# Values of three slots and one gate's columns in Strassen pairs, and the last attention beside the second gate

## The chip, the cores and the metric

The kernel runs on one core of a Trainium2 chip. Its engines work side by side, each through its own list of instructions in order: TensorE (PE in the profile; its weight loads are PEld) multiplies matrices, VectorE (DVE) and ScalarE (ACT) work on elements, GpSimd (POOL) and SyncE (SP) here only issue DMA transfers. An engine waits for another through semaphores. Matmuls write to PSUM, which has eight banks of 128 x 512 float32 values; everything else lies in SBUF. The metric is the device time of one execution in microseconds (us); the time before is 1420.82 us, the median of three runs from 1420.28 to 1421.73.

## The reference

One layer of a decoder on 256 tokens of width 2048, in float32:

```python
u = rmsnorm(h, g_mix_pre)
proj = u @ w_in        # q, k, v of 12 + 4 heads of 128, and two gates of 2048 columns
ya = dilated_mixture_attention(q_a, k_a, v_a) @ w_branch_a   # 3 groups of 4 heads, softmax
yb = stick_breaking_attention(q_b, k_b, v_b) @ w_branch_b    # 4 heads
mix = (sigmoid(gate_a) * ya + sigmoid(gate_b) * yb) @ w_out
h = h + rmsnorm(mix, g_mix_post)
f = (gelu(conv(u2 @ w_up)[:5632]) * conv(u2 @ w_up)[5632:]) @ w_down   # u2 = rmsnorm(h)
h = h + rmsnorm(f, g_ffn_post)
h = h + sigmoid(h @ w_ple_gate) * (p @ w_ple_in)
```

The heads are taken in four slots: slot s has head s of each of the three dilated groups and head s of the stick-breaking branch, so that each slot has four q columns, four k columns and four v columns, each 128 wide.

## The kernel before

**Products in three parts.** Every float32 factor is split into a high part that TensorE takes at full rate and a low remainder; a product is high x high + high x low + low x high. The weights come from HBM as one stream of items, each 128 x 1024 (eight blocks of 128 x 128) in the order in which TensorE uses them. For an item SP loads `raw` (five buffers), ScalarE makes the high part (`high`, line 246) and VectorE the low part (`low`, line 312), into a ring of seven buffers.

**Order.** The order of the work is written out by hand. TensorE asks for the next item, which calls `tick(i)`; there the work that was put off with `defer` is issued, one stage of each waiting job per tick, then the high part of item i + 6, then the low parts up to item i + 5, and then the deferred work of VectorE (it goes ahead of the low parts only when more than two jobs still wait in the list). `lows` also issues the loads, up to five raw buffers ahead of what has been split.

**Strassen pairs.** Where a group has eight columns of 128, two tiles of the inner dimension (k1, k2), two halves of the tokens and two halves of the columns make a 2 x 2 by 2 x 2 product. `gate_groups` (Winograd's form of Strassen) does it in 7 instead of 8 products of 128 x 128 x 512. It needs four combinations of token tiles, made once by `combine(p)` and used by every gate group, and two sums of weights per pair: an item of the first sum, which comes by DMA (SP loads one summand, POOL adds the other; `add_ahead`, `sum_to`, lines 279 and 285), and an item of the second sum, which VectorE makes of it (lines 265 and 266, `weight_sums`). Their lows are line 306. The sums by DMA are put into free quarters of `gh`, the room of the transposed input x. At the end joins (line 995) put the seven products together.

**The stages around the change.** For each slot: eight columns of q and k (`mm`, lines 393 and 395; a column takes one of four PSUM banks in turn, and its evacuation `qk_evac` is deferred), then the four columns of v (`v_units`, lines 725 to 727, with tokens as the stationary side), which are evicted at once by ScalarE and VectorE. The attention of a slot is a generator of eight steps. Six are called between the k-tiles of the slot's v (`STEPS`), two in the next slot's columns (`PACE`); for slot 0 it is two and six. After slot 3 come the first four columns of gate a, beside which the last attention ends, and of gate b (`by_token`), the combinations, the branches' projections, and then three gate groups of eight columns, each with four pairs and eight plain k-tiles. The output projection has a group of its own with six pairs; the token sums of its pairs are made by `gathered(p)`, and the weight sums by `sum_early`.

**Banks.** While attention runs, four banks (`pm1`) serve the columns in turn, and four (`pat`: `S` of two banks, `po`, `z`) serve attention.

Of the kernel before, what the change touches and what calls it, by code (L numbers as in the profile page):

```python
# [14 lines left out]
T = 256  # L15
# [3 lines left out]
NS = 4  # L19
# [15 lines left out]
PAIRS = 4  # L35
OUT = 6
# [4 lines left out]
TURNED = {("qk", s, 1): 3 for s in (2, 3)}  # L41
# [3 lines left out]
STEPS = [(11, 15)] + [(1, 3, 3, 11, 11, 15)] * 3  # L45
PACE = {1: (1, 1, 2, 2), 2: (2,), 3: (2,)}


def _plan():
# [19 lines left out]

    for s in range(NS):  # L70
# [6 lines left out]
    o = 3 * (WA + WB)  # L77

    for j in range(0, KT, 4):
        gates = [[("w_in", o + kind * KT + n) for n in range(j, j + 4)] for kind in range(2)]  # L80
        if j == 0:
            add(("ga", j), gates[0], KT, single)
# [44 lines left out]
def _pairs(group):  # L127

    key = group[0]
    if key[:2] == ("pairs", "out"):  # L130
        return OUT
    if key[0] == "gates" or key[:2] == ("pairs", "pg"):
        return PAIRS
# [3 lines left out]
def _plain():  # L137
    return [k for k in range(KT) if k % 8 >= PAIRS]
# [10 lines left out]
def hybrid_block_kernel(ctx: ExitStack, tc: tile.TileContext, head, gx, xt, pT, convp, bias, masks, gains, w, out):  # L149
# [21 lines left out]
    for g in _plan():  # L171
        if g[0] == "pad":
            short.append(used // 8)
        if _pairs(g):
            assert used % 8 == 0
            before = 14 - 2 * _pairs(g) if g[0][:2] in (("pairs", "pg"), ("pairs", "out")) else 0
            while len(stream) < used // 8 + before + 2 * len(sums_of):
                stream.append(len(stream) - 2 * len(sums_of))
            for p in range(_pairs(g)):
# [3 lines left out]
                if g[0][0] == "pairs" and p < DSUM[g[0][1]]:  # L183
                    early_sums.append(i)
# [6 lines left out]
    gate_sums = sorted(sums_of)[:3 * PAIRS]  # L191
# [56 lines left out]
    def weight_sums(i):  # L248
# [4 lines left out]
        if i not in raw:  # L253
            if n == 0 or a in by_dma:
                x = mps["mp"].tile([128, 1024], F32, name="wsum", tag="wsum")
# [13 lines left out]
    def add_ahead(*ms):  # L269


        for m in ms:
            if m < len(gate_sums):
                k = (4, 12, 0, 8)[m % PAIRS]
                sum_to(gate_sums[m], gh[:, G + k * T:G + (k + 4) * T])
# [26 lines left out]
    def low(i, a=0, b=1024, src=None):  # L302
        if i in sums:
# [3 lines left out]
            if sums[i][1] and sums[i][0] in gate_sums:  # L307
                add_ahead(gate_sums.index(sums[i][0]) + PAIRS)
# [181 lines left out]
    pTs = keep.tile([128, 2, 2 * T], F32R, name="pTs")  # L490
# [224 lines left out]
    def v_units(s):  # L715
        biases[s] = ab.tile([128, 1152], F32, name="bi")
        nc.sync.dma_start(biases[s], bias[s])
        pv = [bank() for _ in range(2)]
# [21 lines left out]
    def attention(s):  # L740
# [10 lines left out]
        P = []  # L751
        for t in range(2):
# [8 lines left out]
            e = ab.tile([128, 3 * n], F32, name=f"e{t}")  # L761
# [78 lines left out]

    def att_step():
# [24 lines left out]
    gates = {}  # L866
    pt = [temp("t", 2) for _ in range(2)]
    for k in range(2):
        nc.sync.dma_start(pt[k], pT[:, k])
        defer((None, None), (None, None), (lambda k=k: usplit(pTs, k, pt[k], low=False), lambda k=k: ulow(pTs, k, pt[k])))  # L870
# [29 lines left out]
    def turn_merged(j, o):  # L900
# [7 lines left out]
        def part(low):  # L908
            for n in range(2):
# [7 lines left out]
    idt = tmp.tile([128, 128], F32, name="idt", tag="ga", bufs=3)  # L917
# [3 lines left out]

    spare = [("s", 2), ("s", 2), ("gb", LATE + 1), ("gb", LATE + 1), ("gb", LATE + 1),
             ("ga", LATE + 1), ("ga", LATE + 1), ("t1", 2), ("t1", 2),
             ("ln", 1), ("ms", 1), ("t", 2), ("t", 2),
             ("s2", 2), ("s2", 2), ("y", 1)]
    S1, S2, S3, S4, A22 = range(5)
    comb, halves_of = [], []

    def combine(p):
        ks, y = (p, p + 8), []  # L930

        def act():
            y.append(mp.tile([128, 6, 128], F32, name="comb"))
            for n, k in enumerate(ks):
                ACT.activation(y[0][:, (5, S4)[n]], h[:, k, :H], AF.Copy, scale=gain(0, k))

        def dve():
            x = y[0]
            DVE.scalar_tensor_tensor(x[:, S3], h[:, ks[0], H:], gain(0, ks[0]), rho, op0=OP.mult, op1=OP.mult)
            DVE.scalar_tensor_tensor(x[:, A22], h[:, ks[1], H:], gain(0, ks[1]), rho, op0=OP.mult, op1=OP.mult)  # L940
            DVE.tensor_tensor(x[:, S1], x[:, S3], x[:, A22], OP.subtract)
            DVE.tensor_tensor(x[:, S2], x[:, S1], x[:, 5], OP.subtract)
            DVE.tensor_tensor(x[:, S3], x[:, 5], x[:, S3], OP.subtract)
            DVE.tensor_tensor(x[:, S4], x[:, S2], x[:, S4], OP.add)
            p == PAIRS - 1 and add_ahead(*range(2, PAIRS))

        def split(low):
            for n in range(4):
                if not low:
                    if not halves_of:  # L950
                        tag, bufs = spare.pop(0)
                        x = tmp.tile([128, 2, 1 + (tag in ("s2", "t")), 128], F32R, name="sp", tag=tag, bufs=bufs)
                        halves_of.extend(x[:, :, i] for i in range(x.shape[2]))
                    comb[p].append(halves_of.pop(0))
                    ACT.activation(comb[p][n][:, 0], y[0][:, n], AF.Copy)
                else:
                    DVE.tensor_tensor(comb[p][n][:, 1], y[0][:, n], f(comb[p][n][:, 0]), OP.subtract)
        comb.append([])
        defer((act, dve), (lambda: split(False), lambda: split(True)))

    def three_wide(ps, x, w, first=False, last=False):
        for n, (i, j) in enumerate(((0, 0), (0, 1), (1, 0))):
            PE.matmul(ps, x[i], w[j], start=first and n == 0, stop=last and n == 2, skip_group_check=True)  # L963

    def gate_groups(j, merged):
# [4 lines left out]

        def tokens(k, t):
            return [u[:, k, i * T + t * H:i * T + (t + 1) * H] for i in range(2)]
# [88 lines left out]
    for j in range(0, KT, 4):  # L1061
        if j:
            ga, gb = gate_groups(j, merged)
        else:
            for kind in ("ga", "gb"):
                ps = [bank() for _ in range(2)]
                for _ in by_token((kind, j), ps, u, (2, 2) if kind == "ga" else ()):
                    att_step()
                if kind == "ga":
                    while stages:  # L1070
                        att_step()
                    at_sc.close()
                    pat_sc.close()
                    pm_sc, pm = scope("pm", space=PSUM)
                    banks["of"] = [(pm1, 4), (pm, 4)]
                    banks["n"] = 0
                    mg_sc, mp = scope("mp")
                    mps["mp"] = mp
                    mg = mp.tile([128, KT, 2 * T], F32R, name="mg")
                    ga = gate("ga", ps)  # L1080
                    rho = tmp.tile([128, H], F32, name="rho", tag="y")
                    DVE.reciprocal(rho, R[:, :H])
# [636 lines left out]
```

## Time and profile before

| | |
|---|---|
| median of three runs | 1420.82 us (1420.28 to 1421.73) |
| profiled execution, its time | 1420.48 us |
| its span | 1418.7 us |
| PE, DVE, ACT, POOL busy | 1412.8, 1188.6, 867.7, 74.7 us |
| slot 1: columns, values | 73.9 to 122.8 us, 122.8 to 148.7 us |
| slots 2 and 3, values | 195.5 to 221.3 us, 268.1 to 294.0 us |
| first columns of the gates | 294.0 to about 338 us |
| three gate groups (with the branches between them) | 350.9 to 497.8 us |
| output projection | from 508.7 us |

A row of the timeline reads: start in us, length in us, engine, line, operation, what is written <- what is read, shape, count; in brackets the idle time of the engine ahead of it and what ended that. A row of a table by stage has the stage's bounds and length, and each engine's busy time with its number of instructions, TensorE's clock, the share of time in which the DMA engines were busy, and what they moved. A row of the view of waits gives who waited for whom, in total, how often, and the longest. A wait is put down to what came last by the profile.

### The profile page before, as it was taken

The page shows a single profiled execution, that of the slowest core. Times are in us where ns is not written, and L with a number is a line of the kernel's source. Part 1 is how long each engine was busy: PE and PEld are TensorE (multiplying, and loading weights), DVE is VectorE, ACT ScalarE, POOL GpSimd, SP SyncE. Part 2 cuts the span into 40 slices and gives each one's busy share as a digit, 9 for nine tenths or more (in the row PEclk, how much of TensorE's full clock was granted, in tenths as well). Part 3 has the DMA queues.
Part 4 walks back from the last instruction along what each step waited for, and adds up shares of the span by engine and source line. Part 5 has one row for each costly group of instructions (what it writes and reads, how often), then busy time and mean ns, then how long its engine had stood idle before and what let it go on. Part 6 is the DMA issues. An engine that isn't in the chain of part 4 may idle for free.

```text
span 1418.7 us, 20516 instructions
## 1 busy us (share of the span) xinstructions
PE 1412.8 (100%) x7343; PEld 1209.5 (85%) x7343; DVE 1188.6 (84%) x1865; ACT 867.7 (61%) x1319; POOL 74.7 (5%) x89
## 2 busy tenths in 40 slices
PE   9999999999999999999999999999999999999998
PEld 8888888888888887898888888888888888888887
DVE  7876666568898899879999788997889978899798
ACT  7665555466656657666666566655566556566564
POOL 0000000002110020000000010000000001000000
PEclk9999999999999999999999999999999999999999
DMA  7754746469976796877876886377863778728775
GB/s 290 268 172 153 250 150 222 152 218 268 298 222 218 254 289 163 299 265 232 254 210 214 266 263 214 102 259 239 260 221 101 248 251 254 233 95 284 245 223 193
DMA packets 100390, 319.59 MB, mean 225 GB/s; under 512 B 11072, under 2 KB 11712, under 8 KB 100160
## 3 DMA queue, kind: packets, MB, share of 16 engines
q1 hardware_dynamic: 88192, 296.25, 61.2%
q0 software_dynamic: 12096, 22.03, 9.0%
q8 instruction: 58, 0.95, 0.3%
q14 instruction: 44, 0.36, 0.1%
HBM read 312.99 MB, written 5.24 MB: 224 GB/s over the span
## 4 chain that ended last, share of the span: by engine, by line
PE 97%; DVE 2%; issue 1%; ACT 0%; DMA 0%; SPq 0%; DVEq 0%
PE mm L963 35%; PE mm L393 29%; PE mm L395 15%; PE mm L727 2%; PE mm L725 2%; PE mm L726 2%; PE mm L883 2%; PE mm L882 2%; PE mm L881 2%; DVE lo L306 1%; DVE lo L312 0%; PE S L393 0%; PE mm L1236 0%; PE mm L415 0%; PE mm L414 0%
## 5 line engine op out<-in xcount | busy, mean ns | idle before, releaser
L312 DVE TENSOR_TENSOR lo<-raw,hi 128x1024 fp32r<-128x1024 f32 (+1 forms) x498 | 575.2, 1173 | 75.3 <-ACT hi L246 70.0
L393 PE MATMUL mm<-u,hi 128*128 128x512 f32 x1796 | 624.8, 392 | 0.0
L246 ACT ACTIVATE hi<-raw 128x1024 fp32r<-128x1024 f32 (+1 forms) x498 | 499.1, 1016 | 168.3 <-DMA raw<-in_w 56.2
L395 PE MATMUL mm<-u,lo 128*128 128x256 f32 x1782 | 499.1, 280 | 0.0
L393 PEld LDWEIGHTS mm<-u,hi 128*128 128x128 f32 x1796 | 335.1, 187 | 72.0
L395 PEld LDWEIGHTS mm<-u,lo 128*128 128x128 f32 x1782 | 336.8, 189 | 1.2 <-DVE lo L312 0.5
L963 PE MATMUL mm<-hi,ft 128*128 128x512 f32 x504 | 162.6, 389 | 0.0
L963 PE MATMUL mm<-hi,u 128*128 128x512 f32 (+1 forms) x492 | 155.4, 387 | 0.1
L451 ACT ACTIVATE t<-mm 128x256 f32<-128x256 f32 x116 | 44.1, 380 | 134.1 <-PE mm L395 134.1
L963 PEld LDWEIGHTS mm<-hi,ft 128*128 128x128 f32 x504 | 94.6, 188 | 19.9 <-DVE ff L1153 0.3
L963 PEld LDWEIGHTS mm<-hi,u 128*128 128x128 f32 x492 | 91.5, 188 | 18.8 <-DVE u L1563 0.9
L963 PE MATMUL mm<-lo,ft 128*128 128x512 f32 x252 | 98.4, 391 | 0.0
L285 POOL DMA_DIRECT2D tsum<-in_w x56 | 49.4, 1020 | 865.3 <-DMA tsum<-in_w 309.0
L963 PE MATMUL mm<-lo,u 128*128 128x512 f32 (+1 forms) x246 | 94.7, 385 | 0.0
L454 DVE TENSOR_TENSOR s<-mm,t 128x256 f32<-128x256 f32 x116 | 48.9, 422 | 52.5 <-ACT t L451 52.5
L963 PE MATMUL mm<-hi,mixed 128*128 128x512 f32 x240 | 83.7, 389 | 0.0
L242 ACT ACTIVATE hi<-wsum 128x512 fp32r<-128x512 f32 x84 | 51.3, 629 | 45.9 <-DVE wsum L265 35.5
L963 PE MATMUL mm<-hi,mg 128*128 128x512 f32 x196 | 62.7, 390 | 0.0
L1415 ACT ACTIVATE cv<-cpad,cw 128x256 f32<-128x256 f32 x88 | 52.5, 597 | 12.4 <-DVE cpad L1410 12.3
L963 PEld LDWEIGHTS mm<-lo,ft 128*128 128x128 f32 x252 | 47.3, 188 | 10.6 <-DVE lo L306 1.1
L306 DVE TENSOR_TENSOR lo<-wsum,hi 128x512 fp32r<-128x512 f32 x84 | 54.0, 684 | 1.5 <-ACT hi L242 1.5
L963 PEld LDWEIGHTS mm<-lo,u 128*128 128x128 f32 x246 | 46.3, 188 | 9.4 <-DVE lo L306 0.4
(328 smaller groups left out, 1877.1 us busy)
## 6 DMA issues: line engine op xcount, KB each, us to landing
raw<-in_w SPq DMA_DIRECT2D x458, 512.0 KB, 4.4
tsum<-in_w POOLq DMA_DIRECT2D x56, 256.0 KB, 7.3
raw<-in_w SPq DMA_DIRECT2D x44, 256.0 KB, 3.2
tsum<-in_w SPq DMA_DIRECT2D x22, 512.0 KB, 5.1
gh<-in_w SPq DMA_DIRECT2D x12, 512.0 KB, 5.8
gh<-in_w POOLq DMA_DIRECT2D x24, 256.0 KB, 7.5
hd<-in_head SPq DMA_DIRECT2D x6, 576.0 KB, 7.4
tsum<-in_w SPq DMA_DIRECT2D x12, 256.0 KB, 6.6
```

What stands on the lines that cost most here:

```text
L242: ACT.activation(hi[i][:, n * 512:(n + 1) * 512], x, AF.Copy)
L246: ACT.activation(hi[i][:, a:b], raw[i][:, a:b] if src is None else src, AF.Copy)
L285: nc.gpsimd.dma_start(x, w[stream[i] + 1 - NE][:, 512:], accum_op=OP.add)
L306: DVE.tensor_tensor(lo[i][:, to], x, f(hi[i][:, to]), OP.subtract)
L312: DVE.tensor_tensor(lo[i][:, a:b], raw[i][:, a:b] if src is None else src, f(hi[i][:, a:b]), OP.subtract)
L393: PE.matmul(ps, wh, rhs, start=first, stop=last, skip_group_check=True)
L395: PE.matmul(ps[:, :T], wl, rhs[:, :T], start=False, stop=last, skip_group_check=True)
L451: ACT.activation(t1[0], ps[:, T:], AF.Copy)
L454: DVE.tensor_tensor(out, ps[:, :T], t1[0], OP.add)
L725: PE.matmul(pv[t], xh, wh, start=kt == 0, stop=False)
L963: PE.matmul(ps, x[i], w[j], start=first and n == 0, stop=last and n == 2, skip_group_check=True)
L1415: ACT.activation(y, c[:, 2:], AF.Identity, scale=cw[:, n, 2:3], bias=cw[:, n, 3:4])
```

## The change

Slot 0's values stay as they were. The values of slot 1 and the first four columns of gate a become one group of eight columns; the values of slots 2 and 3 become another, worked off after the columns of slot 2. Each has ten plain k-tiles first, with the six attention steps between them, and then three Strassen pairs. The combinations are made in slot 1's columns, in one tile of their own; the quarters of x that they need are loaded at slot 0, and the sums by DMA for these pairs are started from slot 1 on. A new function `v_and` works such a group off; it takes all four banks for plain results and attention's four for the products. Its joins, its ends and the split of V (`to_v`) are deferred, in this order. The values of slot 3 wait in a tile and are split after slot 3's third column. The two attention steps that were called after a slot's first column are called after its second. Slot 3 has no value group any more, so its attention runs beside the first columns of gate b in eight steps, after k = 1, 3, 3, 8, 8, 11, 14, 14. Gate a's first columns lie ready as logits, and only their sigmoid is left there. In the output projection the fifth and sixth `gathered` are called ahead of the pairs, and the loads of the last two weight sums later.

The core of the diff:

```diff
-STEPS = [(11, 15)] + [(1, 3, 3, 11, 11, 15)] * 3
-PACE = {1: (1, 1, 2, 2), 2: (2,), 3: (2,)}
+STEPS = [(11, 15)] + [(1, 3, 3, 11, 11, 15)] * 2 + [(1, 3, 3, 8, 8, 11, 14, 14)]
+PACE = {1: (1, 1, 2, 2), 2: (0, 2), 3: (0, 2)}
...
-        add(("v", s), [head("v", s, c) for c in range(4)], KT, single)
+        v = [head("v", s, c) for c in range(4)]
+        if s == 0:
+            add(("v", s), v, KT, single)
+        elif s < NS - 1:
+            w8 = v + [head("v", s + 1, c) if s == 2 else ("w_in", o + c) for c in range(4)]
+            plan.append((("pairs", "v", s), w8, whole(_plain(VPAIRS)) + paired([(p, p + 8) for p in range(VPAIRS)])))
...
+    rooms = [4, 12, 0] * 2 + [4, 12, 0, 8] * 3
...
+    def v_and(s, other):
+
+        assert next(plan)[0] == ("pairs", "v", s)
+        c = {n: bank() for n in ((1, 1), (0, 0), (0, 1), (1, 0))}
+        ks = _plain(VPAIRS)
...
+        w2 = [item() for _ in range(2)]
+        todo = [(k, w, t) for t in range(2) for k, w in zip(ks, w2)] + [(k, None, t) for k in ks[2:] for t in range(2)]
+        for n, (k, w, t) in enumerate(todo):
+            if w is None:
+                w = w2 if t else item()
+                w2 = w
+            half(k, w, t)
+            for _ in range(STEPS[s].count(n)):
+                yield
+        o = {(0, 0): sq.rearrange("p a t -> p (a t)"), (1, 0): ab.tile([128, 512], F32, name="v")}
+        x = other()
+        o[0, 1], o[1, 1] = x[:, 0], x[:, 1]
+        defer((lambda: ACT.activation(o[1, 1], c[1, 1], AF.Copy, scale=Rc[:, 1:2]), None))
...
+        for p in range(VPAIRS):
+            m = [[x[:, 0], x[:, 1]] for x in comb[p]]
+            first, last = p == 0, p == VPAIRS - 1
+            w11, w22 = item()
+            three_wide(P1, tokens(p, 0), w11, first, last)
+            if last:
+                ACT.activation(o[0, 0], P1, AF.Copy, scale=Rc[:, 0:1])
+            three_wide(c[0, 1], m[S4], w22, False, last)
+            q, t3 = item()
+            three_wide(P5, m[S1], q, first, last)
+            three_wide(P7, m[S3], t3, first, last)
+            t2, t4 = item()
+            three_wide(c[1, 0], tokens(p + 8, 1), t4, False, last)
+            three_wide(P6, m[S2], t2, first, last)
+            w21, _ = item()
+            three_wide(c[0, 0], tokens(p + 8, 0), w21, False, last)
+
+        def joins():
+            scaled_add(o[0, 1], P6, 0, o[0, 0])
+            scaled_add(o[0, 0], c[0, 0], 0, o[0, 0])
+            scaled_add(o[1, 0], P7, 0, o[0, 1])
+            DVE.tensor_tensor(o[1, 1], o[1, 0], o[1, 1], OP.subtract)
+            scaled_add(o[0, 1], P5, 0, o[0, 1], OP.subtract)
+            scaled_add(o[1, 1], P5, 0, o[1, 1], OP.subtract)
+
+        def ends():
+            for t, n in ((0, 1), (1, 0)):
+                scaled_add(o[t, n], c[t, n], t, o[t, n])
+        defer((None, joins))
+        defer((None, ends))
+        to_v(s, o[0, 0], lambda: o[1, 0])
+        out_of[s] = x
...
+    nc.sync.dma_start(gh[:, :G + 4 * T], gx[:, :G + 4 * T])
     for s in range(NS):
-        if s == 2:
-
-            nc.sync.dma_start(gh[:, :G + EARLY * T], gx[:, :G + EARLY * T])
+        if s == 1:
             nc.sync.dma_start(gcol, gx[:, 2 * KT:3 * KT])
+            DVE.reciprocal(rho, R[:, :H])
+            DVE.tensor_tensor(rho, rho, R[:, H:], OP.mult)
+            add_ahead(0, 1)
         for c in range(8 if s else 0):
...
             qk_evac(s, c, ps)
+            s == 1 and c % 2 == 0 and combine(c // 2)
+            if (s, c) == (3, 2):
+                v3 = out_of[2]
+                to_v(3, v3[:, 0], v3_rest)
+            c == 7 and load_bias(s)
...
-        for _ in v_units(s):
+        for _ in {0: lambda: v_units(0), 1: lambda: v_and(1, first_gate), 2: lambda: v_and(2, other_v)}[s]() if s < 3 else ():
             att_step()
...
+            for _ in by_token(("gb", j), ps, u, STEPS[3]):
+                att_step()
...
+            ga, gb = out_of[1], gate("gb", ps)
+            defer((lambda: ACT.activation(ga, ga, AF.Sigmoid), None))
+            add_ahead(2 * VPAIRS + PAIRS - 1)
...
-    hooks |= {k: lambda p=p: gathered(p) for p, k in enumerate((1, 5, 9), 1)}
-    hooks |= {2: lambda: sum_early(2, sum_tile("ga", 1)), 6: lambda: sum_early(1),
-              10: lambda: sum_early(4, sum_tile("gb", 2)), 14: lambda: sum_early(5, sum_tile("gb", 2))}
+    hooks |= {k: lambda p=p: gathered(p) for p, k in enumerate((1, 5, 9, 13), 1)}
+    hooks |= {2: lambda: sum_early(2, sum_tile("ga", 1)), 8: lambda: sum_early(1)}
...
-    gathered(PAIRS)
+    gathered(OUT - 1)
...
-                 range(14, KT), o[0, 0], {1: lambda: gathered(OUT - 1)})
+                 range(14, KT), o[0, 0], {p: lambda p=p: sum_early(p + PAIRS + 1, sum_tile("gb", 2)) for p in (-1, 0)})
```

More of the change, by code (lines that the diff above doesn't have):

```diff
@@ L35 @@
 PAIRS = 4
+VPAIRS = 3
 OUT = 6
@@ L134, in _pairs, with _plain @@
     return DROWS // 2 if key[0] == "pairs" else 0
-def _plain():
-    return [k for k in range(KT) if k % 8 >= PAIRS]
+def _plain(pairs=PAIRS):
+    return [k for k in range(KT) if k % 8 >= pairs]
 def _order(group):
@@ L175, in hybrid_block_kernel @@
             assert used % 8 == 0
-            before = 14 - 2 * _pairs(g) if g[0][:2] in (("pairs", "pg"), ("pairs", "out")) else 0
+            before = {"pg": 14, "out": 14, "v": KT}.get(g[0][1], 0)
+            before -= before and 2 * _pairs(g)
             while len(stream) < used // 8 + before + 2 * len(sums_of):
@@ L307, in low @@
             if sums[i][1] and sums[i][0] in gate_sums:
-                add_ahead(gate_sums.index(sums[i][0]) + PAIRS)
+                m = gate_sums.index(sums[i][0])
+                add_ahead(*[n for n in range(m + 1, m + PAIRS + 1) if n < len(rooms) and rooms[n] == rooms[m]][:1])
             return
@@ L716, in v_units, with three_wide, tokens, scaled_add @@
+    def three_wide(ps, x, w, first=False, last=False):
+        for n, (i, j) in enumerate(((0, 0), (0, 1), (1, 0))):
+            PE.matmul(ps, x[i], w[j], start=first and n == 0, stop=last and n == 2, skip_group_check=True)
+    def tokens(k, t):
+        return [u[:, k, i * T + t * H:i * T + (t + 1) * H] for i in range(2)]
+    def scaled_add(to, ps, t, x, op=OP.add):
+        DVE.scalar_tensor_tensor(to, ps, Rc[:, t:t + 1], x, op0=OP.mult, op1=op)
+    def load_bias(s):
         biases[s] = ab.tile([128, 1152], F32, name="bi")
@@ L927, in hybrid_block_kernel @@
[L927 to L959, printed above, removed]
@@ L1061, in hybrid_block_kernel @@
     for j in range(0, KT, 4):
+        if j == 4:
+            pTs = keep.tile([128, 2, 2 * T], F32R, name="pTs", tag="pTs")
+            pt = [temp() for _ in range(2)]
+            for k in range(2):
+                nc.sync.dma_start(pt[k], pT[:, k])
+                defer((None, None), (None, None),
+                      (lambda k=k: usplit(pTs, k, pt[k], low=False), lambda k=k: ulow(pTs, k, pt[k])))
         if j:
@@ L1064, in hybrid_block_kernel @@
         else:
[L1065 to L1082, printed above, removed]
-                    DVE.tensor_tensor(rho, rho, R[:, H:], OP.mult)
-                    for p in range(PAIRS):
-                        combine(p)
-                    add_ahead(0, 1)
-                else:
-                    gb = gate("gb", ps)
+            ps = [bank() for _ in range(2)]
+            for _ in by_token(("gb", j), ps, u, STEPS[3]):
+                att_step()
+            while stages:
+                att_step()
+            at_sc.close()
+            pat_sc.close()
+            pm_sc, pm = scope("pm", space=PSUM)
+            banks["of"] = [(pm1, 4), (pm, 4)]
+            banks["n"] = 0
+            mg_sc, mp = scope("mp")
+            mps["mp"] = mp
+            mg = mp.tile([128, KT, 2 * T], F32R, name="mg")
+            ga, gb = out_of[1], gate("gb", ps)
+            defer((lambda: ACT.activation(ga, ga, AF.Sigmoid), None))
+            add_ahead(2 * VPAIRS + PAIRS - 1)
         for kind, src in (("ba", yT[:, :NS]), ("bb", yT[:, NS:])):
```

101 lines of the change are left out of this document (73 added, 28 removed).

## The prediction

> **What bounds the kernel now.** I read the page first: busy times and slices, then the chain of waits, then busy time by stage, then the timeline of each engine at the places that the change touches.
>
> ```profile
> span 1418.7 us, 20516 instructions
> ...
> PE 1412.8 (100%) x7343; PEld 1209.5 (85%) x7343; DVE 1188.6 (84%) x1865; ACT 867.7 (61%) x1319; POOL 74.7 (5%) x89
> ...
> PEclk9999999999999999999999999999999999999999
> ...
> PE 97%; DVE 2%; issue 1%; ACT 0%; DMA 0%; SPq 0%; DVEq 0%
> ```
>
> TensorE (PE) is never idle, its granted clock is full in all forty slices, and 97% of the chain is its own matmuls. A busy PE isn't yet a PE at its rate, so I looked at the distance between starts in a value group:
>
> ```profile
> 59.64 0.39 PE L727 MATMUL mm<-hi,u 128*128 128x512 f32 x1
> ...
> 63.95 0.39 PE L725 MATMUL mm<-hi,u 128*128 128x512 f32 x1
> ```
>
> Between these rows lie 19 steps: 4.31 / 19 = **0.2268 us per 512-column matmul** (its 0.39 us is a pipelined length). The view of waits has for PE only these:
>
> ```profile
> PE z L611 <- DVE epsb L580: 1.1, 1, 1.1
> PE mm L1236 <- ACT es L1353: 0.5, 1, 0.5
> PE mm L963 <- DVE lo L306: 0.2, 1, 0.2
> ```
>
> None is in the stages of the values and gates, so every matmul taken away there is worth 0.227 us, and every wait that the change makes costs its full length. The question is what the other engines still have free.
>
> ```profile
> core 0: us, PE busy (x) PEld busy (x) DVE busy (x) ACT busy (x) POOL busy (x), PEclk, DMA share, GB/s
> ...
> 73.90:122.80 48.90, 48.90 (x296) 43.56 (x295) 35.57 (x54) 30.36 (x47) 0.00 (x0) 1.00 0.59 184
> 122.80:148.70 25.90, 25.90 (x132) 21.84 (x130) 16.35 (x26) 16.14 (x24) 0.00 (x0) 1.00 0.44 154
> ...
> 403.50:445.20 41.70, 41.70 (x190) 34.60 (x188) 36.02 (x45) 25.50 (x33) 5.31 (x6) 1.00 0.92 279
> ```
>
> The rows are slot 1's columns, slot 1's values, and one of the gate groups, which already use Strassen pairs. The value groups leave VectorE (DVE) a third of its time; a gate group leaves it 14%, and its DMA share is 0.92 against 0.44. The change turns two groups of the easy kind into the hard kind.
>
> **The change part by part.**
>
> *Matmuls.* A pair of k-tiles takes 7 x 3 matmuls of 512 columns instead of 8 x 3. Six pairs take away 18: 18 x 0.2268 = **-4.1 us**. No other matmul is added.
>
> *Combinations of tokens.* The four `combine` calls move from the first gate to slot 1's columns. One costs VectorE 1.7 us and, a tick later, 0.8 us:
>
> ```profile
> 324.70 0.35 DVE L939 SCALAR_TENSOR_TENSOR comb<-gh,rho 128x128 f32<-128x128 f32 x1
> ...
> 326.38 1.23 DVE L312 TENSOR_TENSOR lo<-raw,hi 128x1024 fp32r<-128x1024 f32 x1
> 327.52 0.89 DVE L957 TENSOR_TENSOR sp<-comb,sp 128x128 fp32r<-128x128 f32 x4
> ```
>
> Slot 1's columns have this cover:
>
> ```profile
> 117.95 0.42 DVE L454 TENSOR_TENSOR s<-mm,t 128x256 f32<-128x256 f32 x1 [1.05 <-ACT t L451]
> ...
> 121.22 1.22 DVE L312 TENSOR_TENSOR lo<-raw,hi 128x1024 fp32r<-128x1024 f32 x1 [0.76 <-ACT hi L246]
> 123.49 0.42 DVE L454 TENSOR_TENSOR s<-mm,t 128x256 f32<-128x256 f32 x1 [1.05 <-ACT t L451]
> ```
>
> A column lasts 123.49 - 117.95 = 5.54 us and leaves VectorE 1.05 + 0.76 = 1.8 us. Combinations need 2.5 us in every second column, so the last four columns have room, but the first four share it with slot 0's attention; I carry some 4 us of lateness out of them and work it down to 1 to 2 us. The low parts run more than 10 us ahead of PE, so no weight is late. What is late next is a bank: the new group takes all four, and the one of the last column is wanted 12 matmuls (2.7 us) after the group begins. Its sum now ends 1.1 us after that (123.49 + 0.42, against 122.80); ahead of it come the fourth combination's split (0.8 us) and the lateness. I put **+0.5 us**; bounds 0 and +2.
>
> *Weight sums, more splits, joins.* A pair has two items of sums more and half an item less. The gate group carries this without a stall, in 41.7 us and with a pair more; so do the new groups: nothing on the path. The additions by DMA go out a stage ahead, from SP and POOL. The third load waits on SP until the last combination has left its room, with weight loads queued behind it; those refill buffers that VectorE empties only after the same combination, so they lose nothing; were they not covered, it would be 2 us. The loads of x move to slot 0, shrink by half, and wait on SP behind weights which VectorE splits 10 us before their use. The rest of the moved loads (p, the mask copy) is small and early: nothing.
>
> *When the values are ready.* Before, ScalarE and VectorE evicted the values in 1.5 us. Now they come out of joins, and the next columns need the banks and the last attention step of the slot needs V after two columns. A gate group shows when joins start. Its pairs take 84 x 0.2268 = 19.05 us. Group two, and group three:
>
> ```profile
> 403.47 0.39 PE L963 MATMUL mm<-hi,u 128*128 128x512 f32 x1
> ...
> 430.56 1.23 DVE L312 TENSOR_TENSOR lo<-raw,hi 128x1024 fp32r<-128x1024 f32 x1 [1.07 <-ACT hi L246]
> 431.71 0.74 DVE L995 SCALAR_TENSOR_TENSOR gb<-mm,Rc,ga 128x512 f32<-128x512 f32 x1
> ...
> 456.08 0.39 PE L963 MATMUL mm<-hi,u 128*128 128x512 f32 x1
> ...
> 471.65 6.55 DVE L312 TENSOR_TENSOR lo<-raw,hi 128x512 fp32r<-128x512 f32 x6
> 479.41 1.23 DVE L312 TENSOR_TENSOR lo<-raw,hi 128x1024 fp32r<-128x1024 f32 x1 [1.21 <-ACT hi L246]
> 480.55 0.75 DVE L995 SCALAR_TENSOR_TENSOR gb<-mm,Rc,ga 128x512 f32<-128x512 f32 x1
> ...
> 483.45 2.35 DVE L312 TENSOR_TENSOR lo<-raw,hi 128x1024 fp32r<-128x1024 f32 x2
> ```
>
> The pairs end at 422.5 and 475.1, the joins (L995) start 9.2 and 5.4 us later, and in both a low part stands right ahead of them. `tick` puts the low of the sixth item after the pairs before the join. That item's buffer is one of five; its load is issued only when the first item after the pairs has been split. So the join waits for: that split, a landing, a high (1.06 us) and a low (1.14 us from start to start). How long the landing is, the two groups differ in; the loads issued around the pairs' ends took (group two, then three)
>
> ```profile
> DMA to landing us min/median/max: 7.4/8.5/11.9
> ...
> DMA to landing us min/median/max: 3.4/4.8/5.0
> ```
>
> Group two has sums for the next group in flight; group three has none. The new groups do load sums, at the same rhythm, but the last is issued about 7 us ahead of the pairs' end and not 4.6, with three pairs and not four. I take 6.0 us; bounds 4.8 and 8.5.
>
> [...]
>
> Call the pairs' end E. The first item's split ends at E - 1.7 in group three (472.3 + 1.1 = 473.4); in a new group VectorE comes out of ten plain items, with its queue empty, and I estimate E - 3.8 (not before E - 4.6, when the ring of seven lets it). Join: E - 3.8 + 6.0 + 1.06 + 1.14 + 0.15 = **E + 4.6**; bounds E + 2.6 and E + 9.2. Six join steps at 0.725 (480.55 to 483.45 are four), a low, two ends, a low and the low of V: 4.35 + 1.14 + 1.45 + 1.14 + 0.6 = 8.7, so V is whole at E + 13.3. PE wants it after two columns, at E + 11.1 and two matmuls: E + 11.3. **A stall of 2.0 us in each group**; bounds 0 and 6.6. Half of it may show earlier, at the second column, whose bank the second join step frees (E + 6.1 against E + 5.5). Twice: **+4.0 us**.
>
> *The last attention.* Beside the second gate it runs its sums after k = 8 and no longer after 11.
>
> ```profile
> 268.15 0.39 PE L725 MATMUL mm<-hi,u 128*128 128x512 f32 x1
> ...
> 275.93 0.38 PE L773 MATMUL z<-q,k 128*128 128x128 f32 x2
> ...
> 283.50 0.56 DVE L785 TENSOR_TENSOR l<-l,l 128x384 fp32r<-128x384 f32 x1 [0.59 <-ACT l L784]
> ...
> 287.08 0.51 PE L793 MATMUL z<-l,tri 128*128 128x384 f32 x2
> ```
>
> From the group's start to the end of `l2`'s low part are 284.06 - 268.15 = 15.9 us, one unbroken chain through ScalarE and VectorE. PE came for it at 18.9 us; three k-steps (18 matmuls, 4.1 us) earlier is 14.85. **+1.05 us**; bounds 0 (VectorE is emptier there) and 1.3.
>
> *The output projection.* The fifth and sixth token sums (`gathered`) move ahead of the pairs, where VectorE has a hole; in the pairs PE is held twice:
>
> ```profile
> 533.12 1.23 DVE L312 TENSOR_TENSOR lo<-raw,hi 128x1024 fp32r<-128x1024 f32 x1 [2.89 <-ACT hi L246]
> ...
> 558.55 0.39 PE L963 MATMUL mm<-hi,mg 128*128 128x512 f32 x1
> 559.07 0.50 PE L963 MATMUL mm<-lo,mg 128*128 128x512 f32 x1
> ...
> 564.00 0.39 PE L963 MATMUL mm<-hi,mg 128*128 128x512 f32 x1
> 564.54 0.50 PE L963 MATMUL mm<-lo,mg 128*128 128x512 f32 x1 [0.16 <-DVE lo L306]
> ```
>
> The steps from 558.55 (0.52) and from 564.00 (0.54) stand for 0.23 each, so 0.6 us are lost there, and with the slow steps beside them and one at 562.4 it is 1.05 us. The moved 2.6 us of VectorE covers that: **-1.05 us**; bounds -1.05 and 0.
>
> *Sum.* -4.1 + 0.5 + 4.0 + 1.05 - 1.05 = +0.4 us on a span of 1418.7; the profiled execution took 1420.48, and the median of the runs is 0.34 above it: 1420.82 + 0.4 = **1421.2 us**.
>
> **Rivals.**
>
> *Faster: the loads land as in group three, or sooner.* For it: DMA share 0.44 ahead of the groups. Against it: the sums that fly. With 4.8 us the stall is 0.8; with 3.4 it is gone. Then -4.1 - 1.05 + 1.05 + 0.5 gives 1417.2, and 1415.7 if the waits on the last column's bank and on `l2` are covered too.
> [...]
>
> *Slower: the loads land as in group two.* For it: the same sums in the same queue. 8.5 us in place of 6.0 makes each stall 4.5 us: 1420.82 + 5.4 = 1426.2. It decides from 7.3 us of landing on, where the sum passes +2.9.
>
> *Slower in another way: VectorE stays late through slot 1's columns,* because the first four have no idle time for two combinations and the two steps of rho; PE then waits 3 to 4 us for the last column's bank and for attention: about 1424.5. Against it stand the 1.8 us in each later column.
>
> **How the numbers follow.** A measurement of this kernel tells some 0.2% (2.8 us) from no change. Forecast 0.50, own range 1418.2 to 1424.0; faster rival 0.30; landing as in group two 0.12; VectorE late 0.08. Faster: 0.30 and 0.02 of the forecast's edge, 0.32; slower: 0.20 and 0.05 of the other edge, 0.25; within 0.2%: 0.43. The range that leaves out two in ten: 1415.8 to 1426.0.
>
> **What would show it.** Each step has its own place: the value groups of slots 1 and 2 with 18 matmuls fewer at 0.227 us; a gap of PE some 2.7 us into slot 1's values, released by L454's line; gaps at the second column of slots 2 and 3 or at the attention step after it, released by the joins and V's low part; one gap of 1 us at the tri matmul beside the second gate; no gap near 560 us. If the columns after the value groups run without a gap, the forecast is wrong and the faster rival holds; if those gaps are over 3 us each, the second holds.

## The result and the profile after

The changed kernel takes **1431.36 us** (median of six runs, 1429.09 to 1432.73) against 1421.21 us: a ratio of 1.0071, with a 95% interval of 1.0061 to 1.0082. It is slower by 10.2 us, where 1421.2 us with a range of 1415.8 to 1426.0 was forecast. The profiled execution has a span of 1429.4 us, 10.7 more than before; the working below goes by spans.

The page, and the waits of TensorE (who waited <- for whom: us in total, how often, the longest):

```profile
span 1429.4 us, 20628 instructions
...
PE 88%; DVE 6%; DMA 2%; ACT 2%; issue 1%; DVEq 0%; SPq 0%; ACTq 0%
```

```profile
PE mm L405 <- DVE sq L772: 7.6, 2, 4.1
...
PE S L950 <- ACT pt L951: 0.7, 1, 0.7
...
PE S L871 <- DVE e L898: 0.5, 1, 0.5
PE z L927 <- ACT l L918: 0.4, 1, 0.4
```

The chain that was 97% TensorE now runs for a tenth through VectorE, landings of weights (DMA) and ScalarE. Two waits hold nearly all of it: the columns of q and k (L405) wait for `scaled_add` in the joins (L772). Busy time by stage shows where they lie:

```profile
74.00:122.92 48.92, 48.92 (x297) 43.58 (x295) 43.23 (x92) 35.50 (x71) 3.69 (x4) 1.00 0.73 227
122.92:169.14 46.22, 45.76 (x218) 38.08 (x217) 35.39 (x56) 29.36 (x46) 6.17 (x7) 1.00 0.65 196
169.14:221.90 52.76, 48.70 (x277) 42.75 (x276) 37.38 (x51) 25.51 (x36) 0.88 (x1) 0.97 0.70 231
221.90:267.44 45.54, 45.54 (x219) 38.16 (x217) 33.92 (x51) 29.02 (x44) 4.40 (x5) 1.00 0.54 169
267.44:320.52 53.08, 49.53 (x278) 43.48 (x276) 37.98 (x52) 26.66 (x39) 0.86 (x1) 0.94 0.70 229
320.52:350.79 30.27, 29.06 (x152) 24.08 (x151) 18.51 (x30) 18.72 (x29) 0.00 (x0) 1.00 0.40 142
...
519.47:603.33 83.86, 83.86 (x376) 69.52 (x375) 77.09 (x119) 52.01 (x77) 7.41 (x9) 1.00 0.85 267
```

Column by column as in the prediction's table by stage: bounds, length, PE, PEld, DVE, ACT, POOL, the granted clock, DMA share, GB/s. The same stages of before, in the same order of work: slot 1's columns 48.9 us; slots 2 and 3's columns 46.80 and 46.81; the output stage 85.06:

```profile
148.68:195.48 46.80, 46.80 (x279) 41.49 (x277) 30.72 (x42) 23.79 (x35) 0.00 (x0) 1.00 0.66 220
221.34:268.15 46.81, 46.81 (x280) 41.49 (x278) 30.72 (x42) 23.79 (x35) 0.00 (x0) 1.00 0.61 199
...
508.65:593.71 85.06, 84.78 (x375) 69.27 (x374) 76.99 (x119) 52.23 (x77) 7.04 (x8) 1.00 0.85 261
```

The three value stages of slots 1 to 3 and the gates' first columns took 25.86 + 25.86 + 71.87 = 123.59 us before (122.82 to 148.68, 195.48 to 221.34, 268.15 to 340.02) and take 46.22 + 45.54 + 30.27 = 122.03 now. So the ledger of the span is:

| | us |
|---|---|
| values and gates' first columns, 122.03 - 123.59 | -1.6 |
| columns of slot 2, 52.76 - 46.80 | +6.0 |
| columns of slot 3, 53.08 - 46.81 | +6.3 |
| output stage, 83.86 - 85.06 | -1.2 |
| from there to the end, 826.07 - 824.99 (the same instructions) | +1.1 |
| start, and the branches and gate groups | +0.1 |
| sum | +10.7 |

Behind the output stage the same instructions last 824.9 to 826.1 us in the eleven traces of this case, so the +1.1 there is scatter. The loss lies in two stages which got no work of their own, and there the clock fell too (0.97 and 0.94). In the first of them, the timelines of TensorE and of VectorE:

```profile
174.67 0.28 PE L407 MATMUL mm<-u,lo 128*128 128x256 f32 x1
179.00 0.47 PE L405 MATMUL mm<-u,hi 128*128 128x512 f32 x1 [4.06 <-DVE sq L772]
```

```profile
173.54 1.23 DVE L324 TENSOR_TENSOR lo<-raw,hi 128x1024 fp32r<-128x1024 f32 x1 [1.21 <-ACT hi L255]
176.12 1.23 DVE L324 TENSOR_TENSOR lo<-raw,hi 128x1024 fp32r<-128x1024 f32 x1 [1.35 <-ACT hi L255]
177.26 0.74 DVE L772 SCALAR_TENSOR_TENSOR ga<-S,Rc,sq 128x512 f32<-128x512 f32 x1
178.11 0.75 DVE L772 SCALAR_TENSOR_TENSOR sq<-mm,Rc,sq 128x512 f32<-128x512 f32 x1
```

TensorE stops at the second column (174.8 = E + 5.6, with E the group's end at 169.14), until the second join step has read that column's bank. The joins begin at 177.26 = E + 8.1, right behind the low part of the sixth item, as the prediction had it; only that low part is late. The transfers issued around the pairs' end (163.0 to 168.5 us; line, queue, operation, count, KB each, median us to landing) tell why:

```profile
raw<-in_w SPq DMA_DIRECT2D x5, 512.0 KB, 9.3
gh<-in_w POOLq DMA_DIRECT2D x3, 256.0 KB, 7.8
```

9.3 us is more than the worst that the prediction allowed (8.5). The load of the sixth item itself was issued at 165.59 us and landed at 174.93, also 9.3 us later; in the second group, issued at 263.89, it took 8.8. The second row is the weight sums of the next group, the additions that GpSimd (POOL) issues.

### The profile page after: what moved, and what is told of

It is laid out like the page before. It is cut to its first block, busy times and chain, and to the rows that moved or that the text cites. A ratio compares the mean times of both kernels' runs of the same rounds, so it can differ in the third digit from the quotient of the medians.

```text
span 1429.4 us, 20628 instructions
## 1 busy us (share of the span) xinstructions
PE 1414.2 (99%) x7325; PEld 1209.4 (85%) x7325; DVE 1216.6 (85%) x1917; ACT 879.6 (62%) x1344; POOL 85.3 (6%) x101
## 4 chain that ended last, share of the span: by engine, by line
PE 88%; DVE 6%; DMA 2%; ACT 2%; issue 1%; DVEq 0%; SPq 0%; ACTq 0%
PE mm L766 37%; PE mm L405 27%; PE mm L407 14%; DVE lo L324 2%; DMA raw<-in_w 2%; PE mm L1028 1%; PE mm L1026 1%; PE mm L1027 1%; DVE lo L317 1%; ACT hi L255 1%; PE mm L860 1%; PE mm L859 1%; PE mm L858 1%; DMA bi<-in_bias 1%; PE S L405 0%
## 5 line engine op out<-in xcount | busy, mean ns | idle before, releaser
L405 PE MATMUL mm<-u,hi 128*128 128x512 f32 x1796 | 629.1, 394 | 7.6 <-DVE sq L772 7.6
L405 PEld LDWEIGHTS mm<-u,hi 128*128 128x128 f32 x1796 | 337.2, 188 | 81.3 <-ACT hi L255 8.2
L766 PE MATMUL mm<-hi,u 128*128 128x512 f32 (+1 forms) x676 | 216.6, 389 | 0.1
L766 PEld LDWEIGHTS mm<-hi,u 128*128 128x128 f32 x676 | 126.0, 188 | 25.8 <-DVE u L1662 0.9
L766 PE MATMUL mm<-lo,u 128*128 128x512 f32 (+1 forms) x338 | 130.7, 387 | 0.1
L466 DVE TENSOR_TENSOR s<-mm,t 128x256 f32<-128x256 f32 x116 | 48.9, 421 | 46.4 <-ACT t L463 46.4
L766 PEld LDWEIGHTS mm<-lo,u 128*128 128x128 f32 x338 | 63.6, 188 | 13.6 <-DVE lo L317 0.8
L766 PEld LDWEIGHTS mm<-lo,ft 128*128 128x128 f32 x252 | 47.3, 188 | 10.7 <-DVE lo L317 1.1
L296 POOL DMA_DIRECT2D gh<-in_w x36 | 31.9, 996 | 400.0 <-DVE lo L324 94.6
```

The source lines that it names most:

```text
L296: nc.gpsimd.dma_start(x, w[stream[i] + 1 - NE][:, 512:], accum_op=OP.add)
L405: PE.matmul(ps, wh, rhs, start=first, stop=last, skip_group_check=True)
L466: DVE.tensor_tensor(out, ps[:, :T], t1[0], OP.add)
```

## The experiments

**The next group's sums put off.** The sums that are in flight at the end of slot 1's group (169 us) are wanted by pairs that begin at 253.2 us; here they start in the next slot's columns.

```diff
-                add_ahead(*[n for n in range(m + 1, m + PAIRS + 1) if n < len(rooms) and rooms[n] == rooms[m]][:1])
+                nxt = [n for n in range(m + 1, m + PAIRS + 1) if n < len(rooms) and rooms[n] == rooms[m]][:1]
+                later.extend(nxt) if m < 2 * VPAIRS else add_ahead(*nxt)
...
             qk_evac(s, c, ps)
+            s > 1 and c in (2, 4, 6) and add_ahead(later.pop(0))
```

> The changed kernel, except that the weight sums of the next group that come by DMA are no longer started as each pair is split but in the next slot's columns (after columns 2, 4 and 6), long after the joins. Theory A (the loads behind the pairs land late, in 8 to 11 us, because these sums are in flight with them): landings fall to 4 to 6 us, the joins start about 3 to 5 us earlier, both waits of TensorE (4.2 and 3.7 us) shrink to under 1 us, the half-clock stretches behind them go, and the time falls by 9 to 12 us, to 1419 to 1422. Theory B (the six raw loads that VectorE sets free within 5 us at the end of the pairs are late from their own number, sums or not): landings stay above 8 us, waits above 3 us, time within 2 us of the changed kernel's 1431.4.

1422.22 us; ratio to before 1.0007 (0.9998 to 1.0016). The transfers around the pairs' end (164.4 to 168.6 us here and in the next such views; in this window the changed kernel's loads take 10.1):

```profile
raw<-in_w SPq DMA_DIRECT2D x4, 512.0 KB, 5.2
```

The joins begin at 173.11, 3.7 us after this kernel's group (169.38). What is left of TensorE's waits:

```profile
PE po L872 <- DVE vs L848: 1.3, 2, 0.7
...
PE S L951 <- ACT pt L952: 0.7, 1, 0.7
PE mm L406 <- DVE sq L773: 0.6, 1, 0.6
PE S L872 <- DVE e L899: 0.6, 1, 0.6
```

Theory A holds: some 9 us of the 10.2 were the sums in flight. Without them the four raw loads of this view, issued within 3.4 us as in the changed kernel, land in 5.2 us, so their own number was not the trouble.

**The joins first.** The sums are left in flight, but the joins no longer wait behind the low part of their tick.

```diff
-        late = len(waiting) > 2
+        late = len(waiting) > 2 or joins_in[0] > 0
+        joins_in[0] -= 1
...
+        joins_in[0] = 1
         defer((None, joins))
```

> The changed kernel, except that VectorE does the joins of the two value groups ahead of the low part of that tick instead of behind it; the loads are left as they are. [...] Theory B (the order is not what holds the joins, the products or the bank are): waits of 3.7 to 4.2 us stay, 1431. [...]

1428.38 us; 1.0051 (1.0036 to 1.0066). In the changed kernel the fifth item's low part ends 2.5 us ahead of the joins (173.54 + 1.23 against 177.26), so joins ahead of the sixth item's should, by the author's estimate, shorten the waits at the bank from 4.2 and 3.7 us to 1.7 and 1.2. They shrink to 1.3 and 1.1 us (steps; the view shows the idle part), and the next wait in the chain takes their place, the one for V in the attention step after the second column:

```profile
PE po L874 <- DVE vs L850: 3.7, 2, 1.9
PE mm L407 <- DVE sq L774: 2.1, 2, 1.2
```

The clock fell behind both waits for V (0.998 over this run's span of 1427.6 us, 1.000 in the kernel before). So the gain is 3.0 us by the medians and not the 7 to 9 that the author expected of shorter waits and full clock, 1422 to 1424 us (the intervals of the two ratios overlap a little, so its size is rough): the estimate forgot what was late next.

**Additions apart from loads.** SyncE loads the first summand of each next sum when it did, and only the additions to it are to come later.

```diff
+                if m < 2 * VPAIRS:
+                    i, to = gate_sums[nxt[0]], room(rooms[nxt[0]])
+                    nc.sync.dma_start(to, w[stream[i] - NE])
+                    later.append((i, [to[:, :512], to[:, 512:]]))
+                else:
+                    add_ahead(*nxt)
...
+            s > 1 and c in (2, 4, 6) and add_to_sums(*later.pop(0))
```

> The changed kernel with only half of the sums' traffic put off: SyncE still loads the first summand of each next sum as the pair is split, but GpSimd's additions to it wait for the next slot's columns. If the plain bytes in flight make the raw loads late, half of them are left, landings are 7 to 8 us and about half of the two waits and of the half-clock stretches stays: 1426 to 1428. If the additions are what is slow (in the changed kernel their queue took 25% of the engines' time for 0.26 MB, the loads' 63% for 1.01 MB), nearly all of the gain of the run without sums comes: 1422 to 1424.

1431.78 us; 1.0079 (1.0063 to 1.0094). This run didn't do what it was made for. Around the pairs' end:

```profile
raw<-in_w SPq DMA_DIRECT2D x4, 512.0 KB, 10.3
gh<-in_w POOLq DMA_DIRECT2D x2, 256.0 KB, 9.5
```

The additions are there as before. Their place in the program had moved, but GpSimd has nothing else in its queue and no wait on the columns, so it issued them as soon as the summands had landed (154.00 and 163.38 us, against 153.58 and 162.54 in the changed kernel). In the next run it has such a wait: a part of each summand is loaded again in the columns.

```diff
+                for n, x in enumerate(to):
+                    nc.sync.dma_start(x[:, :128], w[stream[i] - NE][:, n * 512:n * 512 + 128])
                 add_to_sums(i, to)
```

> As in the run before it, SyncE loads the first summand of each next sum as the pair is split; but now 128 columns of each half of it are loaded again in the next slot's columns, so that GpSimd's addition, which must wait for them, is really held until then (in the run before it nothing held GpSimd: it issued its additions at 154.0 and 163.4 us, as in the changed kernel). If the plain bytes in flight make the raw loads late, landings are 7 to 8 us and half of TensorE's two waits stays: 1426 to 1428. If the additions are what is slow, landings are 5 to 6 us as with no sums in flight, and the time is 1422 to 1424.

1422.35 us; 1.0012 (1.0003 to 1.0021), as with no sums in flight at all.

```profile
raw<-in_w SPq DMA_DIRECT2D x4, 512.0 KB, 5.7
```

So of the sums' two halves it is the additions that make the raw loads late: 9.3 us with them, 5.7 with the plain summands, 5.2 with neither. The two halves do not fly at the same time, though: the last summand had landed at 166.3 us in this run, and the last of the changed kernel's additions lands at 177.7. So these runs don't separate the adding, or GpSimd's queue, from the mere bytes in flight at that moment. The queues' shares in the changed kernel say something on it, while the sixth item's load was in flight (165.59 to 174.93 us; SyncE's queue and then GpSimd's: packets, MB, share of the 16 engines' time):

```profile
q1 hardware_dynamic: 559, 2.03, 57.1%
q0 software_dynamic: 463, 0.85, 49.2%
```

In that stretch a byte of the additions took the DMA engines twice as long as a byte of the loads (49.2 / 0.85 = 58% of their time a MB, against 57.1 / 2.03 = 28%).

**The clock.** The kernel before, with TensorE held at six places of slots 2 and 3's columns by a chain on VectorE (one run, 1449.94 us; only its trace is used).

```diff
+        PE.transpose(ps[:, :128], ident, ident)
+        DVE.tensor_tensor(y[:, :128], ident, ps[:, :128], OP.subtract)
+        for _ in range(n - 1):
+            DVE.tensor_tensor(y, f(u[:, 0]), f(u[:, 1]), OP.add)
+        PE.transpose(ps[:, 128:256], y[:, :128], ident)
```

> The kernel before with six added holds in the columns of slots 2 and 3: a transpose on TensorE, then 1, 4, 6 (slot 2) and 3, 5, 8 (slot 3) operations on VectorE that wait for it, then a transpose that waits for the last; estimated idle time of TensorE 1.0, 3.1, 4.5, 2.4, 3.8 and 5.8 us. If the granted clock falls only after an idle stretch of a certain length, as the changed kernel's waits of 4.2 and 3.7 us suggest against its wait of 0.9 us, the short holds are followed by full clock and the long ones by about half clock for some 4 to 5 us, 2 us of loss each; the boundary should lie between 0.9 and 3.7 us. If the clock falls with any idle time, the short holds show it too, and if it falls for another reason (the pairs' kind of work), none does.

The idle stretches were 0.38, 2.56 and 4.01 us in slot 2 and 1.83, 3.29 and 5.46 in slot 3. Those of 4.01, 1.83, 3.29 and 5.46 us came with a granted clock of 0.50 (from 198.61 to 202.03, 253.23 to 256.64, 270.29 to 273.71 and 287.36 to 294.19 us); with that of 2.56 it stayed 1.00. So in this run the length of the wait alone doesn't decide. Busy time and clock of this kernel around three of the holds, in rows of the length of the shorter half-clock stretches (bounds, length, PE busy, ..., clock, DMA share, GB/s):

```profile
178.13:181.54 3.41, 2.32 (x14) 1.80 (x13) 0.98 (x3) 1.47 (x3) 0.00 (x0) 1.00 0.51 154
181.54:184.96 3.42, 1.95 (x12) 1.72 (x13) 3.35 (x6) 0.27 (x2) 0.00 (x0) 1.00 0.00 0
184.96:188.37 3.41, 3.41 (x22) 2.93 (x21) 2.59 (x3) 1.44 (x2) 0.00 (x0) 1.00 0.77 213
...
249.82:253.23 3.41, 1.58 (x11) 1.20 (x9) 1.87 (x4) 1.33 (x2) 0.00 (x0) 1.00 0.36 132
253.23:256.64 3.41, 3.41 (x12) 2.93 (x12) 3.04 (x5) 0.31 (x1) 0.00 (x0) 0.50 0.41 118
...
283.95:287.36 3.41, 0.00 (x0) 0.00 (x0) 3.24 (x6) 0.00 (x0) 0.00 (x0) 1.00 0.00 0
287.36:290.78 3.42, 2.71 (x9) 2.32 (x10) 3.39 (x5) 0.42 (x1) 0.00 (x0) 0.50 0.18 40
290.78:294.19 3.41, 3.41 (x13) 2.92 (x12) 0.64 (x2) 0.70 (x1) 0.00 (x0) 0.50 0.80 267
```

The hold of 2.56 us (180.45 to 183.01) lies in two of these rows, with TensorE busy for 2.32 of 3.41 and 1.95 of 3.42 us, and the clock is 1.00 in both and in the next. That of 1.83 us (251.26 to 253.09) lies in one, with TensorE busy for 1.58 of 3.41 us, and in the next row the clock is 0.50: 12 matmuls where 22 go through at full clock (184.96). What in these rows sets the clock isn't shown. In the changed kernel the rows around its two waits are:

```profile
176.35:179.76 3.41, 0.76 (x4) 0.69 (x5) 3.27 (x5) 1.94 (x2) 0.00 (x0) 1.00 1.03 405
179.76:183.17 3.41, 3.41 (x13) 2.93 (x12) 3.41 (x5) 1.92 (x4) 0.00 (x0) 0.50 0.52 213
...
271.92:275.33 3.41, 1.32 (x8) 0.91 (x6) 2.10 (x3) 1.06 (x1) 0.00 (x0) 1.00 1.07 312
275.33:278.75 3.42, 1.96 (x6) 1.71 (x7) 3.28 (x6) 3.09 (x4) 0.00 (x0) 0.50 1.03 420
278.75:282.16 3.41, 3.41 (x13) 2.92 (x12) 3.41 (x5) 0.80 (x3) 0.00 (x0) 0.50 0.39 137
```

TensorE lost half of its busy time there: (3.41 + 1.96 + 3.41) / 2 = 4.4 us beside the waits of 4.2 and 3.7. Together they are the 12.2 us of the two stages.

**The output stage alone**, in the kernel before:

```diff
-    hooks |= {k: lambda p=p: gathered(p) for p, k in enumerate((1, 5, 9), 1)}
+    hooks |= {k: lambda p=p: gathered(p) for p, k in enumerate((1, 5, 9, 13), 1)}
...
-    gathered(PAIRS)
+    gathered(OUT - 1)
```

> The kernel before, with only the output stage's part of the change (fifth and sixth token sum ahead of the pairs, the last two weight sums loaded later). If the prediction's term is right, TensorE's three waits in the pairs go and the stage lasts 1.05 to 1.2 us less: about 1419.7. If what is won there only moves to the next wait, the time stays at 1420.8.

1419.75 us; 0.9991 (0.9982 to 1.0001). The stage, which was 85.06 us, has no wait left:

```profile
509.59:593.48 83.89, 83.89 (x376) 69.58 (x375) 77.12 (x119) 52.11 (x77) 7.93 (x9) 1.00 0.87 267
```

That is 1.17 us less in the stage and 1.26 in the median. The interval of the ratio just takes in no change, so the stage is what carries this.

**Sums late, and the other waits covered.** The five waits that the first run left are each given time: attention after the third column, one half k-tile later in slot 1, and a new order for the last attention.

```diff
-STEPS = [(11, 15)] + [(1, 3, 3, 11, 11, 15)] * 2 + [(1, 3, 3, 8, 8, 11, 14, 14)]
-PACE = {1: (1, 1, 2, 2), 2: (0, 2), 3: (0, 2)}
+STEPS = [(11, 15)] + [(1, 4, 4, 11, 11, 15), (1, 3, 3, 11, 11, 15)] + [(1, 3, 3, 8, 10, 11, 14, 15)]
+PACE = {1: (1, 1, 2, 2), 2: (0, 0, 2), 3: (0, 0, 2)}
...
+        for stage in (turned(1), sums(), turned(0)) if s == NS - 1 else (sums(), turned(1, 0)) if s else (turned(0), sums(), turned(1)):
```

> The changed kernel with the next group's sums started in the next slot's columns, as in the run that put them off (1422.2 us), and the five waits of TensorE that were left there given cover: the two attention steps after a value group are called after the third column (0, 0, 2) and not the second; in slot 1's group the second and third attention steps one half k-tile later (after the fifth and no longer the fourth); beside gate b the steps of the last attention in another order (the first transposes, then the sums, then the other transposes) and after k = 1, 3, 3, 8, 10, 11, 14, 15. If the waits were all that stood against the 18 matmuls and the output stage's 1.2 us, 0.75 + 0.76 + 0.80 + 0.84 + 1.81 = 5.0 us go and the time is 1417.2, under the kernel before by 0.2 to 0.3%. If they only move to the next step in each chain, it stays at 1420 to 1422.

1418.2 us; 0.9983 (0.9974 to 0.9991). In the view of waits only the one at the start and one behind the output stage are left, which the kernel before has too. With the joins first as well:

> The same, and the joins ahead of the low part of their tick. The wait of 0.8 us for the second column's bank in slot 3 goes (the joins start up to 2.4 us earlier): 0.8 us less than the same kernel without it if that wait is still there, else no difference (within 0.3 us); later low parts may cost something, which would show as waits of weight loads for VectorE's low part.

**1417.68 us; 0.9976 (0.9967 to 0.9986)**: 3.1 us under the kernel before, the best of all. The 0.5 us between the two can't be told from none by their intervals. Its chain, and its stages from slot 1's values on:

```profile
PE 99%; DVE 0%; ACT 0%; issue 0%
```

```profile
123.34:168.85 45.51, 45.51 (x219) 38.17 (x217) 36.49 (x57) 31.24 (x48) 1.76 (x2) 1.00 0.56 166
168.85:216.31 47.46, 47.46 (x278) 41.52 (x276) 35.80 (x50) 23.31 (x35) 4.02 (x5) 1.00 0.86 276
216.31:261.83 45.52, 45.52 (x219) 38.17 (x217) 35.06 (x52) 30.99 (x46) 1.29 (x2) 1.00 0.50 147
...
309.29:337.53 28.24, 28.24 (x151) 24.10 (x150) 17.73 (x28) 17.30 (x27) 0.25 (x1) 1.00 0.52 156
```

Here the change is seen without its waits: 45.51 + 45.52 + 28.24 = 119.27 us, 4.3 less than the 123.59 of before.

**Order alone.** Sums in flight as in the changed kernel, joins first, attention after the third column (the joins' part of the diff, shown above, is left out here).

```diff
-PACE = {1: (1, 1, 2, 2), 2: (0, 2), 3: (0, 2)}
+PACE = {1: (1, 1, 2, 2), 2: (0, 0, 2), 3: (0, 0, 2)}
```

> The changed kernel with its sums in flight as they are, but the joins ahead of the low part of their tick and the two attention steps after the third column (0, 0, 2). With the joins first alone, TensorE waited 1.3 and 1.1 us for the bank and 2.0 and 2.1 us for V, and the clock fell twice: 1428.4. Here the two waits for V should go, and with them the half-clock stretches (1.7 us each): 1428.4 - 4.1 - 3.4 = 1420.9. If the later weight loads run out behind the joins instead, new waits for VectorE's low part appear and the time stays above 1425.

1426.62 us (1424.95 to 1430.73); 1.0048 (1.0029 to 1.0067). The waits for V went, and no wait for low parts came. But those at the bank were longer than with the joins first alone:

```profile
PE mm L407 <- DVE sq L774: 3.6, 2, 2.3
```

Behind one of them the clock fell (0.999 over the profiled run's span of 1423.2 us). Order can't make up for loads that land late. The bank's waits grew from 2.1 us in total to 3.6 because the load that the joins now wait for, that of the fifth item, landed later: 8.7 and 7.7 us after its issue (at 164.31 and 261.33 us), against 7.5 and 7.3 with the joins first alone (165.40 and 263.50). The differences of 1.1 and 0.3 us are the growth of the two waits; why these loads landed later isn't settled. The four runs lie 5.8 us apart. Their granted clocks are 1.000 in the fastest (1424.95 us), 0.999 in those of 1425.15 and 1428.09 and 0.996 in the slowest (1430.73), so the clock goes with a part of that; what the rest is isn't shown.

## Why the prediction was wrong

| term | forecast | measured |
|---|---|---|
| 18 matmuls | -4.1 | -4.0: the -1.6 of the ledger without the 0.6 and 1.8 below (-4.3 in the version with its waits covered) |
| VectorE late at the end of slot 1's columns | +0.5 | not seen; +0.6 in the same stage from another wait |
| joins late, twice | +4.0 | +12.2: waits of 7.9, and 4.4 at half clock |
| last attention | +1.05 | +1.8 |
| output stage | -1.05 | -1.2 |
| the rest | 0 | +1.2, of which 1.1 in unchanged code |
| sum | +0.4 | +10.6 (10.7 by the spans; the rest is rounding) |

**Failed: the landing behind the pairs.** The step was "I take 6.0 us; bounds 4.8 and 8.5"; the two loads that decide took 9.3 and 8.8. The formula around it held: with 9.3 in place of 6.0 it puts the joins at E + 4.6 + 3.3 = E + 7.9 (measured E + 8.1), with 5.2 at E + 3.8 (measured E + 3.7), and attention's want of V, which it put at E + 11.3, came at 180.79 - 169.38 = E + 11.4 in the run with late sums. Only the input was wrong. It was taken between a gate group with sums in flight and one with none, with the argument that "the last is issued about 7 us ahead of the pairs' end". That is so of SyncE's half (162.66 us, E - 6.5). The additions to it come later:

```profile
167.28 0.86 POOL L296 DMA_DIRECT2D gh<-in_w  x1 [2.97 <-DVE lo L324]
169.99 0.88 POOL L296 DMA_DIRECT2D gh<-in_w  x1 [1.84 <-issue]
```

The first goes out 0.7 us after the summand has landed (166.61; it does so in the joins-first and additions-apart runs too, so that VectorE in the bracket is only what came last by the profile), the second 0.3 us after the addition issued at 162.54 has landed (169.68). That is E - 1.9 and E + 0.9; in group two of the kernel before, where the load that the joins wait for took 8.5, it is E + 0.1 and E + 1.2 (422.60 and 423.65). The prediction looked at the half that is early and not at the half that is slow.

**Missing: the clock.** The prediction noted full clock in all forty slices and then costed each wait at "its full length". The two waits here, of 4.2 and 3.7 us, cost more, but not by all of the 4.4 us. The formula with a landing of 9.3 has a stall of 2.0 + 3.3 = 5.3 us, 0.6 + 3.3 = 3.9 of it at the second column's bank and the rest at the attention step that wants V. Only the first part was seen: V was whole at 185.75 us and TensorE came for it at 186.26, in the second group at 283.53 and 284.88. Had half clock not delayed TensorE by 1.7 and 2.7 us, it would have waited there for 1.2 and 1.3. So an estimate of the clock's own price from these rows is 4.4 - 2.5 = 1.9 us. The landing brings the sum to 1420.82 + 0.4 + 6.6 = 1427.8 us, the clock to 1429.7, and the other rows of the table, 2.0 us above their forecasts, to 1431.7. The nearest rival, landing as in group two (1426.2), had the mechanism and nearly the landing, and by the prediction's own sign, gaps of over 3 us each, it is the one that holds; it had neither the clock nor these others.

**Right place, other size: the last attention.** The wait for `l2` at the tri matmul came as forecast (0.52 + 0.42 against 1.05 us). The wait of 0.87 us at the second transposes, whose bank ScalarE still reads (L950 <- ACT L951), was not seen: the two transposes come after k = 8 and 11, three k-tiles apart, where it was four (11 and 15). The order of steps in the two versions with the other waits covered removes both.

**Right number, other cause: the start of slot 1's values.** The prediction had VectorE come late out of the combinations and hold the last column's bank. No wait at that bank is in the trace. The 0.6 us are lost at the third attention step (L871 <- DVE L898), and VectorE stood idle ahead of it until the attention's bias table had landed:

```profile
129.12 0.56 DVE L898 TENSOR_TENSOR e<-S,bi 128x384 f32<-128x384 f32 x1 [2.23 <-DMA bi<-in_bias]
```

That load was issued at 121.89 us, right behind a summand, and took 7.1 us; in the kernel before it was issued at 120.53 and took 4.5. The prediction has no term for it, so that its 0.5 us came out is luck.

**Right: the matmuls, the output stage, and the columns of slot 1,** which took 48.92 us with four combinations in them as without.

## What to carry to other kernels

A load that is issued when it can be issued may still come at the wrong time: the additions by DMA here were wanted some 80 us later and made the loads that were wanted at once nearly twice as long (9.3 against 5.2 us). Before moving work that prefetches, ask what will be waiting for its own loads in that moment, and hold the queue with a real dependency: GpSimd's idle queue issued the additions that had been moved behind the next columns at 154.00 and 163.38 us, against 153.58 and 162.54 where they had stood before. A wait of TensorE can cost more than its length: those of 4.2 and 3.7 us here came with 3.41 and 6.83 us at half clock, 4.4 us of lost busy time, of which an estimated 1.9 was not won back by a shorter wait at the next place. And when a number comes out, look at which wait it is made of.

## What the runs showed of the hardware

In the changed kernel the granted clock was 0.50 from 179.76 to 183.17 us and from 275.33 to 282.16, around waits of 4.2 and 3.7 us. In the kernel with six holds a wait of 1.83 us came with 3.41 us at half clock and one of 2.56 us with none. TensorE was busy for 1.58 us of the 3.41 ahead of that stretch, and for 2.32 and 1.95 us of the two rows in which the wait of 2.56 lies. What sets the clock isn't shown.

Transfers that add to what is in SBUF, issued by GpSimd, slowed plain 512 KB loads of SyncE's queue from 5.2 to 9.3 us, and from 165.59 to 174.93 us of the changed kernel took the DMA engines twice as long a byte (49.2% of their time for 0.85 MB, against 57.1% for 2.03 MB). With the plain summands alone, most of which had landed before, it was 5.7. What part of the slowing is the adding and what part the bytes isn't shown.

One thing isn't explained: in the version with the joins first, the columns of slots 2 and 3 last 47.46 us with no wait and full clock, against 46.80 before, with the 512-column steps at 236 ns and not 230. The version with late sums alone has 236 ns on average in the first two of these columns and 230 behind the attention steps after them, with the same sums in flight; the version with the other waits covered and the joins not first has 235 to 236 there, so the joins' place isn't what sets it. From one block of attention's matmuls to the next the steps of these versions keep one of two patterns: 230 ns throughout, or about 232, 241 and 235 in turn. The changed kernel's trace has both, 236, 232 and 240 ns in turn from 170 to 174 us and 230 from 191 to 195. The difference costs 1.3 us in all, and what sets it isn't known.
